# The delta net's inverse: 32-row block products become 128-row products with zeros

## The chip, the cores and the metric

One Trainium2 chip, one of its cores. The metric is the device time of one execution in microseconds (us), as the median of repeated executions. The core has five engines with their own queues: TensorE (PE in the profile, its weight loads PEld), VectorE (DVE), ScalarE (ACT), GpSimd (POOL) and SyncE (SP, which issues most DMAs).

## The reference

The kernel computes a two-layer trunk on a sequence of 1024 positions and width 1024. Layer 0 mixes with a gated delta net, layer 1 with retention; each is followed by a convolutional feed-forward block and layer norms. The change lies in the delta net alone, in its triangular solve:

```python
kk = jnp.where(strict, jnp.einsum('bhncd,bhnmd->bhncm', kb, k) * decay, 0.0)
rhs = jnp.concatenate([v * beta[..., None], kb * jnp.exp(gc)[..., None]], axis=-1)
sol = lax.linalg.triangular_solve(kk + eye, rhs, left_side=True, lower=True, unit_diagonal=True)
...
def step(state, inp):
    v_new = u_n - jnp.einsum('bhck,bhkv->bhcv', w_n, state)
    o = einsum(q_n * exp(g_n), state) + einsum(qk_n, v_new)
    state = state * exp(g_last) + einsum(k_n * exp(g_last - g_n), v_new)
```

There are 8 heads. The reference uses chunks of 64 positions; the kernel uses chunks of 128, so each head has 8 chunks, each with a unit lower triangular matrix of 128x128 to invert. The scan then walks through the chunks of a head one after another.

## The kernel before

All delta net work between the first projections and the output projection (about 60 to 620 us) is written as generators ("streams"): `filler` (projections, each a run of 128x512 products), `t_decay`, `t_path`, `t_chain`, `prep`, `dt_half`, `scan`, `tail`. A small planner, `run` (L727), keeps a clock of its own and picks at each step the stream of highest priority that is due. A stream says after each piece how long it must wait (`yield LAT["t1"]`), which event it needs (`after_ev`), or which buffers (`take`, `give`). Each product adds a cost by the length of its last dimension (`COST = {32: 0.067, 64: 0.119, 128: 0.224, ...}`, in `pm`), and a dependency ties every PE instruction to the one before it (`pq`). So the planner's order is PE's order. The order of the other engines is made by a scheduler from the dependencies.

The inverse of a chunk's matrix is built from its four 32x32 diagonal blocks. `t_path` inverts the diagonal blocks of a quad of four heads on VectorE (lines L894 and L896) and leaves them in two tiles, `RX` and its transposed twin `TX`. `t_chain(p)` (from L915) does the rest for a pair of heads, p = 0 to 3; pairs 0 and 1 run together, pairs 2 and 3 together later. I call these two rounds. `R[h]` holds the inverse in the making, `U[h]` the off-diagonal factors, `T0` the transposed diagonal blocks in columns of 64 per chunk. Its steps:

1. Fill. POOL clears R (L922) and one part of T0 (L937). Blocks of RX go into R's diagonal, blocks of TX into T0. For even p ScalarE copies (L932), for odd p VectorE (L930); two of R's four blocks go by POOL (L952).
2. Step 1 ("T,U 32x32"). For the lower block of each 64-row half, o = 0 and 64: `pa[h3] = U[l3, h3]^T T0[l3]`, one product with 32 rows, 32 columns and 32 columns moved for each head, chunk and half: 32 products in a pair, into one PSUM bank. ScalarE copies the result to `xa` (L967).
3. Step 2 ("R,xa" and "xa,R"). `pb[l3] = xa^T R[h3, h3]` for both halves and `pb[h3] = R[h3, h3]^T xa` for the first: 48 products of 32x32x32 in a pair, all into one bank `pb`. For o = 0 the two kinds alternate; for o = 64 the first kind stands alone. VectorE writes the negated results into T0 (L980, one per head) and R (L984, four per head).
4. Step 3 ("T,U 64x64" and "R,xb 64x64"). The same on 64-row blocks, one bank per head, results by ScalarE to `xb` (L994) and by VectorE into R (L1004).

The banks that steps 1 to 3 use are a pool of two (`mm_tile`, bufs=2). `lane` buffers (four) hold RX, TX, T0 and others; `give("lane", 2)` in t_chain frees RX and TX when both pairs of a quad have passed step 1 of the list above. The event ("T0", p) lets `prep` (transposes of v, shown as "cst,qkv") and `dt_half` ("acc<-qkv 128x128" and "acc<-q,qkv", after a load of DT by SP, which also takes a lane buffer) begin; ("R", p) lets `scan` begin.

Of the kernel before, what the change touches and what calls it, by code (L numbers as in the profile page):

```python
# [12 lines left out]
ALU = mybir.AluOpType  # L13
# [7 lines left out]
NCH = S // P  # L21
# [12 lines left out]
def trunk_kernel(ctx: ExitStack, tc, A):  # L34
    nc = tc.nc
    pe, act, dve, pool, sp = nc.tensor, nc.scalar, nc.vector, nc.gpsimd, nc.sync
# [24 lines left out]
    def mm_tile():  # L61
        return ps.tile([P, HALF], F32, tag="mm", name="mm", bufs=2)
# [13 lines left out]
    def v4(ap):  # L76
        return ap.rearrange("p (c f) -> p c f", f=P)
# [7 lines left out]
    xs = [dr.tile([S, D], F32, tag=f"xs{i}", name=f"xs{i}") for i in range(3)]  # L85
# [612 lines left out]
    U, DT, R, St = {}, {}, {}, {}  # L698
# [4 lines left out]
    events = {}  # L703

    def pq(inst, cost):
        if pin[0] is not None:
            tc.add_manual_dep(inst.ins, pin[0].name,
                              mybir.DependencyInfo(mybir.DependencyClass.NoSync, mybir.DependencyReason.DATA),
                              reason="issue order")
        pin[0] = inst.ins  # L710
        clk[0] += cost
# [3 lines left out]
    def pm(out, lhsT, rhs, start=True, stop=True, cost=None):  # L715
        pq(pe.matmul(out, lhsT, rhs, start=start, stop=stop), cost or COST[out.shape[-1]])  # L716
# [4 lines left out]
    def after_ev(*names):  # L721
        return ("ev", names)

    def emit(name, lat=0.0):
        events[name] = clk[0] + lat
# [40 lines left out]
    def q4s(q4):  # L766
        return slice(q4 * 4, (q4 + 1) * 4)
# [3 lines left out]
    def take(tag, n):  # L771
        while free[tag] < n:
            yield lambda: free[tag] >= n
        free[tag] -= n

    def give(tag, n):
        free[tag] += n
# [131 lines left out]
    def rx(h, n):  # L909
        return R[h][n // 4][:, n % 4 * P:n % 4 * P + P]  # L910
# [4 lines left out]
    def t_chain(p):  # L915
        heads = pairs[p]
        yield after_ev(("X", p // 2))
        yield from take("auh", 4)
        for h in heads:
            R[h] = two("auh", F32, "R")  # L920
            for q4 in range(2):
                pool.memset(R[h][q4], 0.0)  # L922
        yield after_ev(("T", p // 2))
        RX, TX = RTX[p // 2]
        cx = p % 2 * 16
        yield from take("lane", 1)

        def block(out, src):
            if p % 2:
                dve.tensor_copy(out, src)  # L930
            else:
                act.activation(out, src, AF.Copy)  # L932
        T0 = tl("lane", [P, 2, NCH, 64], name="T0")
        lo, hi = slice(0, 64), slice(64, 128)
        for hh, h in enumerate(heads):
            ch = slice(cx + hh * 8, cx + hh * 8 + 8)
            pool.memset(T0[0:32, hh, :, 32:64], 0.0)  # L937
            for b in range(3):
                bs = slice(32 * b, 32 * b + 32)
                cs = slice(32, 64) if b == 1 else slice(0, 32)  # L940
                block(T0[bs, hh, :, cs], TX[bs, :, ch].rearrange("p i c -> p c i"))
        for hh, h in enumerate(heads):
            for q4 in range(2):
                Rv = v4(R[h][q4])
                ch = slice(cx + hh * 8 + q4 * 4, cx + hh * 8 + q4 * 4 + 4)
                for b in range(4):
                    bs = slice(32 * b, 32 * b + 32)
                    src = RX[bs, :, ch].rearrange("p i c -> p c i")
                    if b < 2:
                        block(Rv[bs, :, bs], src)  # L950
                    else:
                        pool.tensor_copy(Rv[bs, :, bs], src)  # L952
        if ("T0", p ^ 1) in events:
            give("lane", 2)
        emit(("T0", p))
        yield LAT["T0"]
        yield from take("t2", 1)
        pa = mm_tile()
        xa = tl("t2", [P, HALF], name="xa")
        for o in (0, 64):  # L960
            l3, h3 = slice(o, o + 32), slice(o + 32, o + 64)
            for hh, h in enumerate(heads):
                for n in range(NCH):
                    c0 = hh * 256 + 32 * n
                    pm(pa[h3, c0:c0 + 32], U[h][l3, n, h3], T0[l3, hh, n, 0:32])
        for o in (0, 64):
            act.activation(xa[o + 32:o + 64], pa[o + 32:o + 64], AF.Copy)  # L967
        yield LAT["t1"]
        pb = mm_tile()
        for o in (0, 64):  # L970
            l3, h3 = slice(o, o + 32), slice(o + 32, o + 64)
            for hh, h in enumerate(heads):
                for n in range(NCH):
                    c0 = hh * 256 + 32 * n
                    pm(pb[l3, c0:c0 + 32], xa[h3, c0:c0 + 32], rx(h, n)[h3, h3])
                    if o == 0:
                        pm(pb[h3, c0:c0 + 32], rx(h, n)[h3, h3], xa[h3, c0:c0 + 32])
        for hh, h in enumerate(heads):
            pv = pb[:, hh * 256:hh * 256 + 256].rearrange("p (c f) -> p c f", f=32)
            dve.tensor_scalar(T0[32:64, hh, :, 0:32], pv[32:64], -1.0, None, ALU.mult)  # L980
            for o in (64, 0):
                l3, h3 = slice(o, o + 32), slice(o + 32, o + 64)
                for q4 in range(2):
                    dve.tensor_scalar(v4(R[h][q4])[l3, :, h3], pv[l3, q4s(q4)], -1.0, None, ALU.mult)  # L984
        give("t2", 1)
        yield LAT["t2"]
        yield from take("t2", 2)
        xb = {}
        for hh, h in enumerate(heads):
            pa = mm_tile()  # L990
            xb[h] = tl("t2", [P, HALF], name="xb")
            for n in range(NCH):
                pm(pa[hi, 64 * n:64 * n + 64], U[h][lo, n, hi], T0[lo, hh, n])
            act.activation(xb[h][hi], pa[hi], AF.Copy)  # L994
        emit(("Ufree", p))
        give("lane", 1)
        yield LAT["t3"]
        for h in heads:
            pb = mm_tile()
            for n in range(NCH):  # L1000
                pm(pb[lo, 64 * n:64 * n + 64], xb[h][hi, 64 * n:64 * n + 64], rx(h, n)[hi, hi])
            pv = pb.rearrange("p (c f) -> p c f", f=64)
            for q4 in range(2):
                dve.tensor_scalar(v4(R[h][q4])[lo, :, hi], pv[lo, q4s(q4)], -1.0, None, ALU.mult)  # L1004
        give("t2", 2)
        emit(("R", p), LAT["mm"])
# [222 lines left out]
    c, z = "c", "z"  # L1229
# [586 lines left out]
    cs = {}  # L1816
# [358 lines left out]
```

## Time and profile before

| what | us |
|---|---|
| median of 3 runs | 2892.94 (2889.35 to 2898.21) |
| the profiled execution, its own time | 2895.01 |
| its span, first to last instruction | 2893.2 |
| PE busy | 2796.5 |
| DVE busy | 2181.8 |
| round 1 of the inverse (pairs 0, 1), steps 1 to 3 | about 261 to 293 |
| round 2 (pairs 2, 3), steps 1 to 3 | about 507 to 541 |
| scan of heads 0 to 3, of heads 4 to 7 | about 304 to 356, 549 to 613 |

In the answers of the trace, a row gives a start and a duration or a busy time; "[x <-y]" is idle time of the engine before the row and what ended it. PEclk is the TensorE clock that was granted, as a share of full speed; a product of fp32 numbers shows as two records on PE, each with a weight load on PEld. A PE record lasts from its start to the modelled end of its results, so records overlap, and the distance between starts tells the rate.

### The profile page before, as it was taken

Reading aid. Unit: us, or ns where it says so; the run is one execution under the profiler, and the core shown is the slowest. Engines: PE = TensorE matmul, PEld = TensorE weight load, DVE = VectorE, ACT = ScalarE, POOL = GpSimd, SP = SyncE. Lnnn points to the kernel's source line nnn. Section 1 sums busy time; section 2 is a strip of 40 time slices with the busy share of each in tenths; the row PEclk is TensorE's granted clock in tenths of the full one; section 3 lists DMA queues with packets and bytes.
Section 4 is the critical chain, followed back from the end, with each engine's and each line's share of the span. In section 5 each row is a group of like instructions: output and inputs, shape, how many; then the busy total and the mean of one; then the engine's idle time right before and its main releaser. Section 6 shows DMA issues by size and latency. Waiting matters only on the chain.

```text
span 2893.2 us, 38921 instructions
## 1 busy us (share of the span) xinstructions
PE 2796.5 (97%) x13594; PEld 2289.9 (79%) x13594; DVE 2181.8 (75%) x3874; ACT 1296.7 (45%) x2387; POOL 484.6 (17%) x509
## 2 busy tenths in 40 slices
PE   7999999999999999999999999999999999999997
PEld 6788887887787777887788887777777788888886
DVE  5787688576788888858687666666789887777779
ACT  4664375344544444545443333222344644444543
POOL 0311231010022333000000001333301023332001
PEclk9998999899999999999999999999999999999999
DMA  7233233174254655845443354665764253434853
GB/s 277 84 99 117 89 129 112 44 241 153 83 179 169 204 181 176 294 150 175 150 142 113 131 197 143 203 188 177 233 221 150 73 197 138 142 132 161 289 182 116
DMA packets 252884, 465.30 MB, mean 161 GB/s; under 512 B 24144, under 2 KB 77776, under 8 KB 252688
## 3 DMA queue, kind: packets, MB, share of 16 engines
q1 hardware_dynamic: 218560, 408.02, 42.8%
q10 hardware_dynamic: 31488, 46.15, 4.3%
q0 software_dynamic: 2640, 8.65, 0.8%
q8 instruction: 107, 1.75, 0.2%
q14 instruction: 89, 0.73, 0.1%
HBM read 346.86 MB, written 115.87 MB: 160 GB/s over the span
## 4 chain that ended last, share of the span: by engine, by line
PE 60%; DVE 21%; DMA 8%; issue 5%; ACT 4%; POOL 1%; SPq 0%; ACTq 0%; DVEq 0%; POOLq 0%
PE acc L716 11%; PE acc L1292 5%; PE acc L1592 4%; PE sc L716 4%; PE acc L110 4%; PE acc L111 4%; PE acc L112 4%; PE mm L716 3%; PE sc L1292 3%; DVE o L1738 2%; DVE wb L90 2%; DMA wr<-in_ffn_up 2%; DMA mvw<-in_ada_w 2%; DVE mm L1346 2%; DVE ada L239 1%
## 5 line engine op out<-in xcount | busy, mean ns | idle before, releaser
L716 PE MATMUL acc<-hT,wh 128*128 128x512 f32 x960 | 301.1, 395 | 0.0
L1592 PE MATMUL acc<-bb,ab 128*128 128x512 f32 x984 | 231.0, 394 | 8.2 <-DVE ab L90 4.4
L89 ACT ACTIVATE ab<-ar 128x512 fp32r<-128x512 f32 x210 | 131.4, 630 | 222.9 <-PE mm L303 49.8
L1592 PEld LDWEIGHTS acc<-bb,ab 128*128 128x128 f32 x984 | 184.2, 189 | 50.0 <-DVE bb L90 4.7
L716 PEld LDWEIGHTS acc<-hT,wh 128*128 128x128 f32 x960 | 183.2, 191 | 36.1
L90 DVE TENSOR_TENSOR ab<-ar,ab 128x512 fp32r<-128x512 f32 x210 | 146.1, 701 | 80.3 <-ACT ab L89 80.1
L1292 PE MATMUL acc<-T,wb 128*128 128x512 f32 x840 | 202.0, 389 | 0.4 <-DVE wb L90 0.4
L716 PE MATMUL acc<-hT,wl 128*128 128x512 f32 x480 | 197.4, 411 | 3.3 <-ACT sq L509 2.1
L89 ACT ACTIVATE wb<-mm 128x512 fp32r<-128x512 f32 x216 | 124.3, 597 | 167.8 <-DVE mm L1346 154.1
L1292 PEld LDWEIGHTS acc<-T,wb 128*128 128x128 f32 x840 | 157.5, 188 | 33.8 <-ACT o L1739 1.2
L90 DVE TENSOR_TENSOR wl<-wr,wh 128x1024 fp32r<-128x1024 f32 x98 | 122.8, 1253 | 76.3 <-ACT wh L89 76.0
L90 DVE TENSOR_TENSOR wb<-wr,wb 128x512 fp32r<-128x512 f32 x162 | 116.3, 719 | 66.1 <-ACT wb L89 66.1
L89 ACT ACTIVATE wh<-wr 128x1024 fp32r<-128x1024 f32 x98 | 103.8, 1060 | 137.4 <-PE acc L716 54.1
L1769 POOL TENSOR_TENSOR o<-o 128x512 f32<-128x512 f32 x80 | 113.0, 1422 | 265.2 <-ACT pc L1362 173.1
L1738 DVE SCALAR_TENSOR_TENSOR o<-g,vc,o 128x512 f32<-128x512 f32 (+2 forms) x176 | 148.3, 852 | 8.2 <-ACT o L1733 7.0
L90 DVE TENSOR_TENSOR wb<-mm,wb 128x512 fp32r<-128x512 f32 x216 | 144.4, 681 | 7.6 <-ACT wb L89 7.6
L89 ACT ACTIVATE wb<-wr 128x512 fp32r<-128x512 f32 x162 | 101.2, 626 | 94.8 <-PE acc L1292 28.5
L1346 DVE TENSOR_TENSOR mm<-wr 128x512 f32<-128x512 f32 x108 | 85.9, 796 | 75.5 <-DMA wr<-in_ffn_up 60.9
L716 PE MATMUL acc<-wh,hT 128*128 128x512 f32 x384 | 134.3, 412 | 1.8 <-DVE vv L90 1.8
L1362 ACT ACTIVATE pc<-acc 128x512 f32<-128x512 f32 x143 | 84.3, 590 | 109.9 <-PE acc L1292 63.4
L239 DVE SCALAR_TENSOR_TENSOR ada<-mvw,e,ada 128x512 f32<-128x512 f32 x140 | 105.3, 752 | 23.4 <-DMA mvw<-in_ada_w 23.0
L110 PE MATMUL acc<-T,wb 128*128 128x512 f32 x292 | 114.4, 392 | 6.1 <-DVE wb L90 6.1
(674 smaller groups left out, 7371.9 us busy)
## 6 DMA issues: line engine op xcount, KB each, us to landing
wr<-in_ffn_up SPq DMA_DIRECT2D x92, 512.0 KB, 3.9
mvw<-in_ada_w SPq DMA_DIRECT2D x80, 512.0 KB, 4.3
ad<-o SPq DMA_DIRECT2D x154, 256.0 KB, 2.3
ar<-ad SPq DMA_DIRECT2D x154, 256.0 KB, 3.9
Br<-in_ffn_down SPq DMA_DIRECT2D x88, 256.0 KB, 3.6
wr<-in_ret_wv SPq DMA_DIRECT2D x32, 512.0 KB, 3.7
ar<-od SPq DMA_DIRECT2D x56, 256.0 KB, 5.2
wr<-in_gdn_wqkv SPq DMA_DIRECT2D x24, 512.0 KB, 3.6
```

The lines of the kernel that those rows point to most:

```text
L89: anchor["sp"] = act.activation(dst_h, src, AF.Copy)
L90: eng.tensor_tensor(dst_l, src, dst_h, ALU.subtract)
L110: mm(acc, wl[:, k], hl[0], start=first, stop=False)
L111: mm(acc, wh[:, k], hl[1], start=False, stop=False)
L112: mm(acc, wh[:, k], hl[0], start=False, stop=last)
L239: dve.scalar_tensor_tensor(a, wr[:, kk], e[:, k:k + 1], a, ALU.mult, ALU.add)
L716: pq(pe.matmul(out, lhsT, rhs, start=start, stop=stop), cost or COST[out.shape[-1]])
L1292: return pe.matmul(*a, skip_group_check=True, **kw)
L1346: dve.tensor_tensor(t, x, y, op)
L1592: return pe.matmul(*args, skip_group_check=True, **kw)
L1738: dve.scalar_tensor_tensor(tv, gv[:, c0 - j:c1 - j], w[:, 2 - j:3 - j], tv, ALU.mult, ALU.add)
L1769: (dve if fp == 0 else pool).tensor_tensor(o[d], o[x], o[y], op)
```

## The change

Only `t_chain` changes.

- T0 is cleared over all 128 rows (POOL, 128x512 per head instead of 32x256), and at first only the blocks of rows 0 to 31 and 64 to 95 are copied in, the second into columns 32 to 63. The remaining block, rows 32 to 63, follows behind step 1.
- Step 1 uses all 128 rows of U and T0: 32 products per pair as before, each with 128 rows, 32 columns of weights and 32 columns moved. What other rows hold meets zeros in T0.
- xa is cleared on POOL first (128x512), so its rows outside the two blocks are zero.
- Step 2 uses all 128 rows, too. One product of xa with two of R's column blocks (64 columns moved) replaces the two products of the halves; the other kind stays. So 16 products in a head, 32 in a pair instead of 48, and they alternate throughout.
- The results of step 2 go into one bank per head instead of one per pair.
- RX and TX are given back behind step 1 and the late block copies, by a new event ("T1", p).

```diff
-            pool.memset(T0[0:32, hh, :, 32:64], 0.0)
-            for b in range(3):
+            pool.memset(T0[:, hh], 0.0)
+            for b in (0, 2):
                 bs = slice(32 * b, 32 * b + 32)
-                cs = slice(32, 64) if b == 1 else slice(0, 32)
-                block(T0[bs, hh, :, cs], TX[bs, :, ch].rearrange("p i c -> p c i"))
+                block(T0[bs, hh, :, 16 * b:16 * b + 32], TX[bs, :, ch].rearrange("p i c -> p c i"))
...
-        if ("T0", p ^ 1) in events:
-            give("lane", 2)
         emit(("T0", p))
...
+        pool.memset(xa, 0.0)
         for o in (0, 64):
-            l3, h3 = slice(o, o + 32), slice(o + 32, o + 64)
+            h3 = slice(o + 32, o + 64)
             for hh, h in enumerate(heads):
                 for n in range(NCH):
                     c0 = hh * 256 + 32 * n
-                    pm(pa[h3, c0:c0 + 32], U[h][l3, n, h3], T0[l3, hh, n, 0:32])
+                    pm(pa[h3, c0:c0 + 32], U[h][:, n, h3], T0[:, hh, n, o // 2:o // 2 + 32])
...
+        for hh in range(2):
+            ch = slice(cx + hh * 8, cx + hh * 8 + 8)
+            block(T0[32:64, hh, :, 32:64], TX[32:64, :, ch].rearrange("p i c -> p c i"))
+        if ("T1", p ^ 1) in events:
+            give("lane", 2)
+        emit(("T1", p))
         yield LAT["t1"]
-        pb = mm_tile()
-        for o in (0, 64):
-            l3, h3 = slice(o, o + 32), slice(o + 32, o + 64)
-            for hh, h in enumerate(heads):
-                for n in range(NCH):
-                    c0 = hh * 256 + 32 * n
-                    pm(pb[l3, c0:c0 + 32], xa[h3, c0:c0 + 32], rx(h, n)[h3, h3])
-                    if o == 0:
-                        pm(pb[h3, c0:c0 + 32], rx(h, n)[h3, h3], xa[h3, c0:c0 + 32])
         for hh, h in enumerate(heads):
-            pv = pb[:, hh * 256:hh * 256 + 256].rearrange("p (c f) -> p c f", f=32)
+            pb = mm_tile()
+            pv = pb.rearrange("p (c f) -> p c f", f=64)
+            for n in range(NCH):
+                xs = xa[:, hh * 256 + 32 * n:hh * 256 + 32 * n + 32]
+                pm(pv[0:32, n], xs, rx(h, n).rearrange("p (b j) -> p b j", j=32)[:, 1::2])
+                pm(pv[32:64, n, 0:32], rx(h, n)[:, 32:64], xs)
...
```

The other rows of the diff are the VectorE writes behind step 2, as many as before and of the same sizes.

What this does to the order on PE at the first round's step 1 stands in the next two fences (T with a number is T0 of a pair, "hT" rows are projections, "cst,qkv" transposes of `prep`, "acc<-qkv" products of `dt_half`). Before:

```order
L716 MATMUL acc<-qkv 128x128 x4
L719 MATMUL acc<-cst,qkv 128x128 x8
L716 MATMUL acc<-hT,wl 128x512
L716 MATMUL acc<-hT,wh 128x512 x2
L716 MATMUL acc<-hT,wl 128x512
L716 MATMUL acc<-hT,wh 128x512 x2
L716 MATMUL acc<-qkv 128x128 x4
L716 MATMUL mm<-T_2178,U 32x32 x32
L716 MATMUL mm<-T_2203,U 32x32 x32
L719 MATMUL acc<-cst,qkv 128x128 x8
L716 MATMUL acc<-hT,wl 128x512
L716 MATMUL acc<-hT,wh 128x512 x2
```

With the change:

```order
L719 MATMUL acc<-cst,qkv 128x128 x8
L716 MATMUL acc<-hT,wl 128x512
L716 MATMUL acc<-hT,wh 128x512 x2
L716 MATMUL acc<-hT,wl 128x512
L716 MATMUL acc<-hT,wh 128x512 x2
L716 MATMUL acc<-hT,wl 128x512
L716 MATMUL acc<-hT,wh 128x512 x2
L719 MATMUL acc<-cst,qkv 128x128 x8
L716 MATMUL acc<-hT,wl 128x512
L716 MATMUL acc<-hT,wh 128x512 x2
L716 MATMUL mm<-T_2178,U 32x32 x32
L716 MATMUL mm<-T_2201,U 32x32 x32
```

The 64 products of step 1 keep their number (the shape shown is that of the result); `dt_half`'s products have moved behind step 2, and transposes and projections ahead of step 1.

ScalarE in the same round, behind its copies into R (L491, L485 and L488 belong to a projection's convolution; "acc" is what a projection left in PSUM). Before:

```order
L485 ACTIVATE raw<-acc 128x512
L488 ACTIVATE oq<-acc,vc 128x512
L932 ACTIVATE T_2178<-TX 32x8x32 x6
L491 ACTIVATE oq<-oq 128x512
L1212 DMA qd<-oq 128x512
L485 ACTIVATE raw<-acc 128x512
L488 ACTIVATE oq<-acc,vc 128x512
L89 ACTIVATE wh<-wr 128x1024
```

With the change:

```order
L485 ACTIVATE raw<-acc 128x512
L488 ACTIVATE oq<-acc,vc 128x512
L491 ACTIVATE oq<-oq 128x512
L932 ACTIVATE T_2178<-TX 32x8x32 x2
L1212 DMA qd<-oq 128x512
L932 ACTIVATE T_2178<-TX 32x8x32 x2
L491 ACTIVATE oq<-oq 128x512
L485 ACTIVATE raw<-acc 128x512
L488 ACTIVATE oq<-acc,vc 128x512
L89 ACTIVATE wh<-wr 128x1024
L1212 DMA qd<-oq 128x512
L932 ACTIVATE T_2178<-TX 32x8x32
```

Two of the six copies into T0 have moved behind step 1, one ahead of each pair's copies to xa, and one L491 has moved ahead of the L485 and L488 that free the next "acc".

PE in the second scan (sc: heads 4 and 5, mm: heads 6 and 7; "qkv,R", "w,DT", "w,U" and "Sn,..." are a chunk's products in turn). Before:

```order
L716 MATMUL sc<-qkv,R 128x128
L716 MATMUL sc<-Sn,qkv 128x128 x2
L716 MATMUL mm<-Sn,qkv 128x128
L716 MATMUL mm<-Sn,q 128x128
L716 MATMUL mm<-Sn,qkv 128x128
L716 MATMUL mm<-Sn,q 128x128
L716 MATMUL sc<-w,DT 128x128
L716 MATMUL sc<-w,U 128x128
L716 MATMUL acc<-hT,wl 128x512
L716 MATMUL acc<-hT,wh 128x512 x2
```

With the change:

```order
L716 MATMUL sc<-Sn,qkv 128x128 x4
L716 MATMUL mm<-Sn,qkv 128x128
L716 MATMUL mm<-Sn,q 128x128
L716 MATMUL mm<-Sn,qkv 128x128
L716 MATMUL mm<-Sn,q 128x128
L716 MATMUL acc<-hT,wl 128x512
L716 MATMUL acc<-hT,wh 128x512 x2
L716 MATMUL sc<-qkv,R 128x128 x2
L716 MATMUL mm<-qkv,R 128x128
```

Before, heads 4 and 5 ran half a chunk apart; with the change they run side by side, as heads 0 to 3 do in the first scan in both kernels, and more of the projections is left for behind the scan. Behind the first products of the output projection PE's order is the same.

More of the change, by code (lines that the diff above doesn't have):

```diff
@@ L964, in t_chain @@
                     c0 = hh * 256 + 32 * n
-                    pm(pa[h3, c0:c0 + 32], U[h][l3, n, h3], T0[l3, hh, n, 0:32])
+                    pm(pa[h3, c0:c0 + 32], U[h][:, n, h3], T0[:, hh, n, o // 2:o // 2 + 32])
         for o in (0, 64):
             act.activation(xa[o + 32:o + 64], pa[o + 32:o + 64], AF.Copy)
-        yield LAT["t1"]
-        pb = mm_tile()
-        for o in (0, 64):
-            l3, h3 = slice(o, o + 32), slice(o + 32, o + 64)
-            for hh, h in enumerate(heads):
-                for n in range(NCH):
-                    c0 = hh * 256 + 32 * n
-                    pm(pb[l3, c0:c0 + 32], xa[h3, c0:c0 + 32], rx(h, n)[h3, h3])
-                    if o == 0:
-                        pm(pb[h3, c0:c0 + 32], rx(h, n)[h3, h3], xa[h3, c0:c0 + 32])
-        for hh, h in enumerate(heads):
-            pv = pb[:, hh * 256:hh * 256 + 256].rearrange("p (c f) -> p c f", f=32)
-            dve.tensor_scalar(T0[32:64, hh, :, 0:32], pv[32:64], -1.0, None, ALU.mult)
-            for o in (64, 0):
-                l3, h3 = slice(o, o + 32), slice(o + 32, o + 64)
+        for hh in range(2):
[4 more added lines that the diff above has]
+        emit(("T1", p))
+        yield LAT["t1"]
+        for hh, h in enumerate(heads):
+            pb = mm_tile()
[4 more added lines that the diff above has]
+                pm(pv[32:64, n, 0:32], rx(h, n)[:, 32:64], xs)
+            dve.tensor_scalar(T0[32:64, hh, :, 0:32], pv[32:64, :, 0:32], -1.0, None, ALU.mult)
+            for o in (32, 0):
                 for q4 in range(2):
-                    dve.tensor_scalar(v4(R[h][q4])[l3, :, h3], pv[l3, q4s(q4)], -1.0, None, ALU.mult)
+                    dve.tensor_scalar(v4(R[h][q4])[2 * o:2 * o + 32, :, 2 * o + 32:2 * o + 64],
+                                      pv[0:32, q4s(q4), o:o + 32], -1.0, None, ALU.mult)
         give("t2", 1)
```

## The prediction

> **What bounds the kernel now.** First the page: the busy times, and the chain that ended last.
>
> ```profile
> PE 2796.5 (97%) x13594; PEld 2289.9 (79%) x13594; DVE 2181.8 (75%) x3874; ACT 1296.7 (45%) x2387; POOL 484.6 (17%) x509
> ...
> PE 60%; DVE 21%; DMA 8%; issue 5%; ACT 4%; POOL 1%; SPq 0%; ACTq 0%; DVEq 0%; POOLq 0%
> ```
>
> PE is busy for 97% of the span and carries most of the chain, so time is gained where PE does the same work faster, and lost where it waits. Next the stretches with their granted clock (columns: stretch and length, busy time and instructions of PE, PEld, DVE, ACT, POOL, then PEclk, DMA share, GB/s).
>
> ```profile
> 240.00:320.00 80.00, 73.47 (x769) 65.37 (x769) 52.68 (x112) 27.82 (x60) 10.13 (x21) 0.89 0.31 102
> 320.00:480.00 160.00, 157.05 (x854) 134.35 (x854) 129.76 (x350) 94.10 (x203) 42.62 (x55) 1.00 0.35 116
> 480.00:620.00 140.00, 132.51 (x1144) 117.60 (x1143) 90.28 (x223) 60.29 (x162) 18.04 (x30) 0.93 0.31 104
> 620.00:2893.00 2273.00, 2213.76 (x9821) 1791.51 (x9819) 1732.64 (x2795) 980.50 (x1701) 375.30 (x339) 1.00 0.51 171
> ```
>
> The clock is full almost everywhere, but not in the two stretches that hold the two rounds of the inverse. Cut at the moments at which it changes, the same view says why:
>
> ```profile
> 134.77:138.18 3.41, 1.35 (x10) 1.31 (x11) 3.19 (x13) 1.18 (x2) 0.00 (x0) 1.00 0.58 230
> 254.25:257.66 3.41, 1.01 (x7) 0.93 (x8) 2.26 (x4) 2.87 (x5) 0.00 (x0) 0.99 0.73 208
> 257.66:261.07 3.41, 3.41 (x13) 2.83 (x11) 3.20 (x5) 0.40 (x1) 0.00 (x0) 0.50 0.70 258
> 261.07:264.48 3.41, 3.41 (x116) 3.38 (x116) 1.74 (x3) 1.20 (x3) 0.00 (x0) 1.00 0.60 192
> 264.48:267.88 3.40, 3.40 (x28) 3.18 (x26) 1.27 (x2) 1.79 (x3) 0.00 (x0) 0.50 0.52 198
> 267.88:271.29 3.41, 3.41 (x172) 3.07 (x171) 1.02 (x4) 0.00 (x0) 0.00 (x0) 1.00 0.43 145
> 271.29:281.53 10.24, 9.56 (x76) 8.57 (x74) 6.62 (x21) 1.18 (x2) 0.00 (x0) 0.50 0.17 57
> 285.02:288.43 3.41, 3.41 (x48) 3.24 (x46) 0.96 (x3) 1.18 (x2) 0.00 (x0) 1.00 0.05 17
> 503.42:506.83 3.41, 1.88 (x16) 1.40 (x15) 2.81 (x5) 1.93 (x10) 0.18 (x1) 1.00 0.31 127
> 506.83:510.24 3.41, 3.41 (x112) 3.24 (x110) 1.05 (x3) 2.65 (x11) 0.00 (x0) 1.00 0.02 5
> 510.24:530.66 20.42, 19.74 (x280) 18.07 (x278) 8.91 (x25) 2.54 (x5) 0.00 (x0) 0.50 0.09 28
> ```
>
> The clock changes on a grid of 3.41 us. Behind 134.77 and 254.25 it fell to half because PE had been busy for 1.35 and 1.01 us of a window; with 1.88 us, from 503.42, it stayed. But it also fell at 264.48, 271.29 and 510.24, behind windows in which PE was busy throughout. What ran there:
>
> ```profile
> 261.10 4.26 PE L716 MATMUL mm<-T,U 32*32 32x32 f32 x128
> 268.22 0.21 PE L716 MATMUL mm<-R,xa 32*32 32x32 f32 x1
> 269.25 1.01 PE L716 MATMUL mm<-R,xa 32*32 32x32 f32 x27
> 271.09 1.60 PE L716 MATMUL mm<-R,xa 32*32 32x32 f32 x29
> 283.30 2.08 PE L716 MATMUL mm<-R,xb 64*64 64x64 f32 x32
> 285.38 2.05 PE L716 MATMUL mm<-T,U 64*64 64x64 f32 x32
> 288.35 1.04 PE L719 MATMUL acc<-cst,qkv 128*128 128x128 f32 x8
> 295.01 1.05 PE L716 MATMUL acc<-qkv 128*128 128x128 f32 x8
> 507.09 4.41 PE L716 MATMUL mm<-T,U 32*32 32x32 f32 x128
> ```
>
> The three windows are filled by 32x32x32 products. Something that sets the clock counts a small product as little work. Two mixed windows of 64x64 products, one of them from 285.02 with 2.3 of 3.41 us of them, kept the clock.
>
> The Trainium skill, page "TensorE: Matmul & The Clock Gate", section "HAM oscillation — how this bites in real kernels", lets the clock fall when PE idles for over about 3.4 us. The windows at 261.07 and 506.83 agree on the length and not on the cause, since PE never idled in them.
>
> **Part 1: the clock.** The change leaves 32 columns of weights but uses 128 rows instead of 32, in steps 1 and 2. What would be counted, the trace doesn't say: if rows in use, a product of the change counts as full (1.0 instead of 0.25); if cells in use, 0.25 instead of 0.06. By the rows above a window of full-size work keeps the clock from a share between 0.40 (1.35 of 3.41) and 0.55 (1.88 of 3.41). So rows would keep it, and cells would not. I take rows: from 267.88 two 32-column blocks ran side by side for a part of the window (64 records from 268.22 to 269.25, 16 ns each, against some 31 ns in the row from 269.25), so more columns were in use, and it fell all the same. That is a leaning, no proof.
>
> What a kept clock is worth: PE's busy time at half clock becomes half. 3.40 + 9.56 + 19.74 = 32.70 us; half is 16.35. The half-clock window from 257.66 follows idle time and stays. Bounds: 0 and 16.4; I take 16.4, and the waits below off it.
>
> **Part 2: the products.** Step 1 keeps 64 products a round (128 records, 33 ns each). Step 2 has 64 products instead of 96. In a head, 8 products move 64 columns; the 32 records from 283.30 with 64 columns take (2.08 − 0.22) / 31 = 0.060 each, so 16 x 0.060 = 0.96 us if the other kind runs beside them, as today, and 1.47 if each waits for the other (16 x 0.032 more). Today a pair takes 64 x 16 + 32 x 31 ns = 2.0 us, 1.0 a head. So 0 at the low end, 0.5 x 8 = 4 at the high end; I take 0, as the two kinds still use different columns.
>
> **Part 3: one bank per head.** Two banks serve, so the third head's step 2 must wait until VectorE has emptied the first's. VectorE and the copies:
>
> ```profile
> 270.37 0.42 DVE L980 TENSOR_SCALAR T<-mm 32x256 f32<-32x256 f32 x1 [2.38 <-PE mm L716]
> 270.80 0.98 DVE L984 TENSOR_SCALAR R<-mm 32x128 f32<-32x128 f32 x4
> 271.80 0.42 DVE L980 TENSOR_SCALAR T<-mm 32x256 f32<-32x256 f32 x1
> 276.31 1.97 PE L716 MATMUL mm<-T,U 64*64 64x64 f32 x16 [0.68 <-ACT xb L994]
> L967 ACT ACTIVATE xa<-mm x8: 587/588/591, 263.2 to 512.1; 32x512 f32<-32x512 f32 x8
> 256.65 0.66 PE L719 MATMUL acc<-cst,qkv 128*128 128x128 f32 x4 [4.24 <-ACT oq L488]
> L932 ACT ACTIVATE T<-TX x12: 629/674/690, 249.3 to 494.9; 32x256 f32<-32x256 f32 x12
> L937 POOL MEMSET T<- x8: 301/302/455, 248.8 to 494.3; 32x256 f32 x8
> L922 POOL MEMSET R<- x16: 522/526/546, 59.1 to 393.6; 128x512 f32 x16
> ```
>
> A head costs VectorE 271.80 − 270.37 = 1.43 us. Counted from the start of step 2: PE does heads one and two until 1.92, VectorE the first until 2.49; PE idles 0.58, does the third until 3.46; VectorE ends the second at 3.92, PE idles 0.49, does the fourth until 4.9. Four `dt_half` products (8 records, 0.9 by the row from 295.01) fill until 5.8; the third bank is free at 5.35, the fourth at 6.78; step 3's first 8 products (half of 2.05) end at 6.8, so both banks come in time. Sum 1.1 us against the 0.68 in the row from 276.31, so 0.4 more in a round, 0.8 in both. Bounds 0 (at half clock PE is behind VectorE) and 3, if VectorE has other work in between.
>
> **Part 4: POOL and ScalarE.** T0's clearing grows from 0.30 to 0.53 us (a clearing of R has the same size), four clearings of xa come in at 0.53 each; POOL is busy for 17% of the span, and ScalarE now turns to L491 first, which covers it. ScalarE's two late copies put 0.67 ahead of each pair's xa: the first pair's is ready 0.67 + 2 x 0.59 = 1.9 us behind its step 1, while PE has 2.1 us of the other pair's step 1 and then 8 transposes and 3 projections (1.04 + 0.7) to do. The second pair's has the same 1.7 and step 2 of the first pair. Nothing, then; without that cover each would cost up to 1.3. The 4.24 us in which PE idles ahead of 256.65 for an L488 on ScalarE stay: four copies and two L491 stand before it in place of six and one. The later give of RX and TX holds back `dt_half`'s loads of DT, whose products stand behind step 2 now and long before the scan; 0, at most 1.
>
> **Part 5: the second scan.** It takes on the pattern that the first has.
>
> ```profile
> 300.00:356.00 56.00, 53.10 (x397) 48.94 (x395) 36.42 (x108) 25.96 (x84) 10.02 (x11) 1.00 0.33 109
> 548.00:600.00 52.00, 50.92 (x381) 47.39 (x381) 31.79 (x94) 24.13 (x81) 4.79 (x4) 1.00 0.25 81
> 600.00:612.00 12.00, 8.95 (x53) 7.26 (x53) 7.15 (x20) 4.12 (x11) 1.01 (x1) 1.00 0.79 256
> ```
>
> PE idles 2.9 us in the first scan and 1.1 in the second: +1.8. The close of the second idles 3.05; more projections are left for behind it, so it may gain or lose 2. I take +1.8, ends −1 and +4.
>
> **Sum.** −16.4 + 0 + 0.8 + 0 + 1.8 = −13.8 us. The profiled execution took 2895.01 and would take 2881.2; the median stands 2.07 lower, so 2879.1.
>
> **Rivals.**
> - *The clock falls all the same*, because cells or columns count: the change doesn't bring what part 1 hopes for. The window from 285.02 speaks neither for nor against it: by cells its 64x64 products count 0.25, and 2.3 of 3.41 us of that with 1.1 of full size make 0.49, which lies above 0.40 too. Then 0.8 + 1.8 remain: 2895.5; with products one after the other and a worse scan close up to 2901.
> - *The clock holds in one round only*, as the grid of 3.41 us falls otherwise over the mix of products and waits: about half of 16.4, so 2892.9 − 8.2 + 2.6 = 2887.3.
> - *Slower: weight loads come into the open.* Each record has its own load. Today's 32x32 loads last 114 ns and hide behind products 33 ns apart:
>
> ```profile
> L716 PEld LDWEIGHTS mm<-T,U 32*32 32x32 f32 x256 | 8.4, 114 | 0.4 <-issue 0.4
> L614 PEld LDWEIGHTS sc<-hT,wab 128*32 128x32 f32 x8 | 0.9, 108 | 1.7 <-DVE hT L90 1.4
> ```
>
>   If a load over all 128 rows can't run beside a product over all rows, each of the 512 records in steps 1 and 2 takes 108 ns; today these steps take 4.3 + 4.5 us in round 1 (from 261.10, and from 268.22 to 272.69) and at most 4.4 + 9 in round 2, with step 2 at half clock. 512 x 0.108 = 55 against 22: +33, about 2926. It decides from 12 ns a record (6.1 us, with the 2.6 above 8.7). Against it: transposes with 128x128 weights come at 1.04 / 8 = 0.13 us each, with 128 columns moved, though their loads also fill all rows.
>
> The Trainium skill, the same page, section "Part 3: Packing small matmuls — row/col tiling", says that a weight load overlaps running products only if its row group differs; by that rule the time would be the 2926. Step 1 contradicts it: all its products of one half sit in the same 32 rows, 33 ns apart.
>
> **How the numbers follow.** The clock holds: 0.50, own range 2875 to 2885 (2892.9 − 16.4 − 1.5, and with 6 us more of waits). It falls: 0.34. One round: 0.07. Weight loads: 0.09. A measurement of this kernel can tell about 0.3%, 8.7 us, from no change. Faster by more: 0.45 of the first case; within: the rest of it, 0.05, with 0.07 and most of the second, 0.31; slower: 0.09 and 0.03 of the second. The range from 2874 to 2900 holds the first three cases but for their ends.
>
> **What would show it.** Right: PEclk 1.0 in the windows of steps 1 to 3; transposes behind step 2 at 1.04 for eight, as from 288.35; short PE waits for VectorE in step 2; a second scan with some 3 us idle. Wrong: PEclk 0.50 behind the "T,U 32x32" rows again; records of steps 1 and 2 over 60 ns apart; a PE wait for xa or for POOL.

## The result and the profile after

The changed kernel takes 2878.12 us (median of 6 runs, 2873.07 to 2881.79) beside 2895.57 for the kernel before (6 runs, 2889.35 to 2899.15): a ratio of 0.9941 with a 95% interval from 0.9924 to 0.9958, or 17.4 us. Measured twice more, each time beside the kernel before on one chip, the ratio was 0.9946 (0.993 to 0.9963) and 0.9945 (0.9931 to 0.9958), about 16 us (15.3 and 14.4 between the medians). The profiled execution took 2881.79 us, with a span of 2880.0 instead of 2893.2.

First the page of the changed kernel, then the answer by stretches with the same columns as in the prediction.

```profile
PE 2784.3 (97%) x13466; PEld 2275.5 (79%) x13466; DVE 2178.8 (76%) x3874; ACT 1297.3 (45%) x2387; POOL 499.3 (17%) x513
```

```profile
240.00:320.00 80.00, 75.00 (x770) 66.73 (x769) 54.53 (x125) 30.94 (x77) 14.69 (x25) 0.98 0.35 114
...
480.00:620.00 140.00, 130.49 (x1122) 115.23 (x1121) 93.73 (x223) 65.56 (x172) 16.92 (x26) 1.00 0.37 130
620.00:2880.00 2260.00, 2202.15 (x9739) 1780.32 (x9737) 1718.42 (x2775) 968.97 (x1682) 385.09 (x338) 0.99 0.51 170
```

PE loses 12.2 us of busy time, and the granted clock of the two stretches with the inverse goes from 0.89 to 0.98 and from 0.93 to 1.00. Cut on the grid of the clock, with one row ahead of step 1 of round 1, three that hold steps 1 and 2 of it, and two of round 2:

```profile
253.70:257.10 3.40, 3.40 (x26) 2.65 (x25) 3.31 (x7) 0.62 (x1) 0.00 (x0) 0.51 0.78 272
257.10:260.50 3.40, 3.40 (x118) 3.38 (x115) 3.33 (x6) 2.15 (x4) 0.00 (x0) 0.99 0.58 162
260.50:263.90 3.40, 3.40 (x75) 2.96 (x73) 2.16 (x6) 2.14 (x4) 0.00 (x0) 1.00 0.35 114
263.90:267.30 3.40, 2.29 (x75) 2.02 (x70) 3.25 (x13) 0.00 (x0) 0.00 (x0) 1.00 0.64 198
497.80:501.20 3.40, 3.40 (x117) 3.40 (x117) 0.62 (x2) 3.15 (x12) 0.00 (x0) 1.00 0.02 7
504.60:508.00 3.40, 2.29 (x78) 2.03 (x74) 3.25 (x12) 0.00 (x0) 0.00 (x0) 1.00 0.18 58
```

Windows full of step 1 (118 and 117 records) no longer bring the clock down, and neither do the windows of step 2, in which PE is busy for only 2.29 of 3.40 us. The half-clock window ahead of step 1, behind an idle PE, is still there. The rows of PE's timeline in step 1 and behind it, and the two waits inside step 2 of round 1:

```profile
256.32 4.28 PE L716 MATMUL mm<-T,U 128*32 128x32 f32 x128
...
264.95 0.22 PE L716 MATMUL mm<-R,xa 128*32 128x64 f32 x1 [0.71 <-DVE R L983]
266.40 0.22 PE L716 MATMUL mm<-R,xa 128*32 128x64 f32 x1 [0.40 <-DVE R L983]
...
268.47 2.07 PE L716 MATMUL mm<-T,U 64*64 64x64 f32 x32
...
497.81 3.94 PE L716 MATMUL mm<-T,U 128*32 128x32 f32 x128
```

The 128-row products come at 3.94 / 128 = 31 ns a record. The rows of step 1 before, 4.26 and 4.41 us, were a little longer because each ends in a half-clock window (from 264.45 and from 510.21). Step 3 (the 64x64 row) no longer waits for xb.

Where the time went is read from one stretch with the same ends in both kernels: from the first record of step 1 in round 1 to the first record of the output projection (L326). Of the kernel before, by the two rounds and the second scan, and as a whole:

```profile
261.10:304.24 43.14, 42.46 (x589) 38.68 (x589) 22.19 (x50) 7.79 (x15) 0.00 (x0) 0.84 0.22 78
304.24:507.09 202.85, 195.63 (x1076) 166.73 (x1075) 163.02 (x422) 117.90 (x267) 52.41 (x78) 1.00 0.35 115
507.09:548.76 41.67, 40.96 (x556) 37.15 (x555) 21.89 (x50) 9.13 (x21) 0.00 (x0) 0.75 0.12 40
548.76:627.90 79.14, 75.02 (x517) 67.66 (x516) 53.53 (x144) 39.68 (x111) 9.59 (x8) 1.00 0.47 160
261.10:627.90 366.80, 354.07 (x2732) 310.21 (x2732) 260.63 (x663) 174.50 (x413) 62.00 (x86) 0.95 0.33 112
```

And of the changed kernel:

```profile
256.32:294.18 37.86, 36.76 (x526) 33.46 (x526) 25.42 (x57) 9.08 (x17) 0.00 (x0) 0.99 0.29 94
294.18:497.81 203.63, 196.08 (x1076) 166.62 (x1074) 163.21 (x419) 117.11 (x265) 53.00 (x80) 1.00 0.34 112
497.81:533.18 35.37, 34.01 (x502) 30.56 (x502) 22.39 (x52) 10.83 (x24) 0.00 (x0) 1.00 0.18 62
533.18:611.60 78.42, 72.49 (x505) 65.42 (x503) 52.52 (x143) 39.40 (x111) 9.15 (x8) 1.00 0.46 162
256.32:611.60 355.28, 339.33 (x2604) 296.06 (x2603) 263.55 (x668) 176.42 (x415) 62.15 (x88) 1.00 0.34 116
```

The stretch is 11.5 us shorter: PE's busy time falls by 14.7, and its idle time (length less busy time) rises from 12.7 to 15.9. In two further profiles of the changed kernel the stretch lasted 354.3 and 353.7 us, so 12.5 and 13.1 less than before; of the kernel before there is one profile. Outside of it the two profiles differ by −4.8 us ahead (256.32 against 261.10) and by +3.1 behind (2268.4 against 2265.3). About 1.5 of the 4.8 belongs to the change (the wait for L488, under POOL and ScalarE below). The rest, and what lies behind, moves between profiles of one and the same kernel too: step 1 began at 256.3, 260.0 and 257.1 us in the three profiles of the changed kernel. Half-clock windows near 45, 58 and 80 us come and go between these three.

### The profile page after: what moved, and what is told of

It is laid out like the page before. It is cut to its first block, busy times and chain, and to the rows that moved or that the text cites. A ratio compares the mean times of both kernels' runs of the same rounds, so it can differ in the third digit from the quotient of the medians.

```text
span 2880.0 us, 38681 instructions
## 1 busy us (share of the span) xinstructions
PE 2784.3 (97%) x13466; PEld 2275.5 (79%) x13466; DVE 2178.8 (76%) x3874; ACT 1297.3 (45%) x2387; POOL 499.3 (17%) x513
## 4 chain that ended last, share of the span: by engine, by line
PE 55%; DVE 21%; DMA 11%; ACT 6%; issue 4%; POOL 1%; SPq 1%; ACTq 0%; DVEq 0%; POOLq 0%
PE acc L716 7%; PE acc L1292 5%; PE acc L1592 4%; PE acc L110 4%; PE acc L111 4%; PE acc L112 4%; PE sc L716 4%; PE sc L1292 3%; DMA mvw<-in_ada_w 3%; PE mm L716 2%; DVE o L1738 2%; DVE qkv L490 2%; DVE wb L90 2%; DVE ada L239 2%; DMA wr<-in_ffn_up 2%
## 5 line engine op out<-in xcount | busy, mean ns | idle before, releaser
L1769 POOL TENSOR_TENSOR o<-o 128x512 f32<-128x512 f32 x80 | 126.3, 1588 | 267.9 <-ACT pc L1362 173.1
```

The source lines that it names most:

```text
L1769: (dve if fp == 0 else pool).tensor_tensor(o[d], o[x], o[y], op)
```

## The experiments

The theory: what holds the clock is the number of rows in use, and the gain is the clock alone. The rivals: cells count; columns count; the new order (one bank per head, late copies, moved products) makes the gain, and the clock follows from it; or the grid fell luckily.

**One shape at a time.** A kernel of its own: thirteen bursts of fp32 products of one shape each, one behind the other, each behind 60 full-size products that bring the clock up. The core of it:

```python
# rows, columns of weights, columns moved, rows of the moving operand that are not zero
BURSTS = [(32,32,32,32), (64,32,32,64), (128,32,32,128), (128,32,32,32), (32,64,32,32), (32,128,32,32),
          (64,64,32,64), (128,64,32,128), (128,128,32,128), (32,32,128,32), (32,128,128,32), (64,64,64,64), (96,32,32,96)]
...
pq(pe.matmul(pt[0:cols, c:c + n], raw[0:rows, k:k + cols], m, start=True, stop=True))
```

> A kernel of its own that computes nothing of the reference: 13 bursts of fp32 products of one shape each (80 to 260 products, planned for some 17 us), each behind 60 full-size products (some 14 us) that bring the clock to 1.0. Shapes as rows x columns of weights, columns moved: 32x32,32; 64x32,32; 128x32,32; 128x32,32 with zeros in 96 of the rows moved; 32x64,32; 32x128,32; 64x64,32; 128x64,32; 128x128,32; 32x32,128; 32x128,128; 64x64,64; 96x32,32. All theories: 32x32 lets the clock fall to 0.50 within two windows of 3.41 us, 128x32 keeps it at 1.0, with or without zeros. If rows in use count: 32x64, 32x128 and the long 32x32 and 32x128 fall too, 128x64 and 128x128 keep it, 64 rows are open. If cells in use count: 32x128 keeps it as 128x32 does (0.25 of the cells each), 64x64 keeps it, 32x64 (0.125) goes as 64x32. Records of one burst come at 30 to 35 ns with 32 columns moved, unless a weight load of 128 rows or 128 columns is slower: then 50 ns or more.

Rows of PE's timeline: start, length, weights as rows*columns, then moving rows x columns; "zm" is the operand that is zero in 96 of 128 rows.

```profile
21.48 24.07 PE L57 MATMUL b<-raw 32*32 32x32 f32 x520
61.92 16.65 PE L57 MATMUL b<-raw 64*32 64x32 f32 x520
92.33 16.65 PE L57 MATMUL b<-raw 128*32 128x32 f32 x520
122.74 16.65 PE L57 MATMUL b<-zm,raw 128*32 128x32 f32 x520
153.14 52.62 PE L57 MATMUL b<-raw 32*64 32x32 f32 x520
222.20 108.50 PE L57 MATMUL b<-raw 32*128 32x32 f32 x520
346.22 51.38 PE L57 MATMUL b<-raw 64*64 64x32 f32 x520
413.72 30.52 PE L57 MATMUL b<-raw 128*64 128x32 f32 x520
457.90 105.35 PE L57 MATMUL b<-raw 128*128 128x32 f32 x520
578.45 29.52 PE L57 MATMUL b<-raw 32*32 32x128 f32 x160
669.52 16.54 PE L57 MATMUL b<-raw 64*64 64x64 f32 x280
```

And the windows of the first burst, before and after the clock fell:

```profile
23.90:27.30 3.40, 3.40 (x112) 3.40 (x109) 0.00 (x0) 0.00 (x0) 0.00 (x0) 0.98 0.02 5
27.30:44.00 16.70, 16.70 (x318) 16.70 (x316) 0.00 (x0) 0.00 (x0) 0.00 (x0) 0.50 0.01 2
```

The clock fell 2.9 to 6.2 us into every burst that has 32 rows (five shapes, with 32, 64 or 128 columns of weights and 32 or 128 moved), and also with 64x64 and 128x128 weights when only 32 columns are moved. It held with 64, 96 and 128 rows of 32 columns, with zeros in three quarters of the rows, with 128x64 weights, and with 64x64 weights when 64 columns are moved. So it isn't columns (32x128 fell), nor cells: 64x32 (an eighth of the array) held and 128x128 (all of it) fell. Nor is it rows alone: by rows, 128x128 was expected to hold. What sets that burst apart is that its products come further apart. From start to start, before the fall, its records stood 112 ns apart, those of 64x64 58, those of 128x64 58, those of 64x32 32. (The counts in the rows of windows include records that began earlier, so length over count comes out a little short.) Records that move 128 columns through 32x32 weights stood 109 ns apart, 0.85 ns for each column. With that, a shape's share is rows/128 times columns moved times 0.85 over the distance. What fell has 0.25 or less (128x128: 0.24; 64x64 with 32 moved: 0.23; the 32-row shapes 0.06 to 0.25). What held has 0.43 or more (64x32: 0.43; 64x64 with 64 moved: 0.47; 128x64: 0.47). That is a rule made after the bursts to fit all thirteen, not a mechanism that a run has shown.

The Trainium skill, page "TensorE: Matmul & The Clock Gate", section "LDWEIGHTS (loading the stationary operand)", gives a weight load a time in ns of its columns divided by 1.2, whatever its rows. The distances here come within 6 ns of it where 32 columns are moved: 112 ns at 128 columns of weights (107 by the page) with 32 rows as with 128, and 58 at 64 columns (53 by the page) with 64 rows as with 128. At 32 columns the records stood 32 ns apart with 32, 64, 96 and 128 rows.

**The new order with 32 rows.** The changed kernel, with its banks and clearings, but the products of steps 1 and 2 over their own 32 rows, so that step 2 again has 96 products a round. PE's order is otherwise the same up to the output projection. On ScalarE the two late copies stand ahead of step 1 again, since its 32 rows no longer read what they overwrite.

```diff
-                    pm(pa[h3, c0:c0 + 32], U[h][:, n, h3], T0[:, hh, n, o // 2:o // 2 + 32])
+                    pm(pa[h3, c0:c0 + 32], U[h][o:o + 32, n, h3], T0[o:o + 32, hh, n, o // 2:o // 2 + 32])
...
-            for n in range(NCH):
-                xs = xa[:, hh * 256 + 32 * n:hh * 256 + 32 * n + 32]
-                pm(pv[0:32, n], xs, rx(h, n).rearrange("p (b j) -> p b j", j=32)[:, 1::2])
-                pm(pv[32:64, n, 0:32], rx(h, n)[:, 32:64], xs)
+            for o in (0, 64):
+                h3 = slice(o + 32, o + 64)
+                for n in range(NCH):
+                    xs = xa[h3, hh * 256 + 32 * n:hh * 256 + 32 * n + 32]
+                    pm(pv[o:o + 32, n, 0:32], xs, rx(h, n)[h3, h3], cost=0.062)
+                    if o == 0:
+                        pm(pv[32:64, n, 0:32], rx(h, n)[h3, h3], xs, cost=0.062)
```

> The changed kernel with its order on PE, its two banks per pair, its clearings and late copies, but steps 1 and 2 over 32 rows as before (24 products a head in step 2, planned at the same cost). If the rows keep the clock: PEclk falls to 0.50 behind step 1 in both rounds, the time goes back by 11 to 16 us, to 2889 to 2894. If the gain is in the new order, the banks or the moved copies: PEclk may fall or not, the time stays at 2876 to 2882.

2895.44 us beside 2890.37, a ratio of 1.0004 (0.9987 to 1.002); the median is 1.4 us above the range that was expected. The windows of the clock, and the stretch from step 1 to the output projection:

```profile
264.70:268.10 3.40, 3.40 (x25) 2.97 (x22) 1.55 (x3) 1.81 (x3) 0.00 (x0) 0.50 0.28 111
271.50:285.10 13.60, 13.60 (x138) 12.70 (x132) 6.35 (x18) 1.55 (x3) 0.00 (x0) 0.50 0.17 58
513.70:517.10 3.40, 3.40 (x33) 3.24 (x31) 1.11 (x2) 1.30 (x3) 0.00 (x0) 0.52 0.02 5
520.70:534.20 13.50, 13.50 (x139) 12.29 (x132) 5.75 (x17) 1.19 (x2) 0.00 (x0) 0.50 0.13 42
...
261.18:629.87 368.69, 354.07 (x2731) 309.94 (x2731) 263.21 (x664) 174.27 (x413) 62.40 (x88) 0.95 0.32 111
```

The half clock is back in both rounds, and PE's busy time in the stretch is the 354.07 us of the kernel before. The new order alone costs 1.9 us of idle time there (14.6 against 12.7). So the gain comes with the 128-row products. In step 2 these are also fewer, 64 in place of 96 a round; this run undoes both and doesn't separate them.

**One step alone at 32 rows.** The first of the two edits above (step 1), then the second (step 2), each by itself.

> The changed kernel with step 1 alone back at 32 rows. If rows count: the clock falls at the window behind step 1 in both rounds and comes back at the earliest one or two windows later; a loss of 3 to 10 us against the changed kernel, its time at 2880 to 2888. If step 2 alone mattered: no fall.

> The changed kernel with step 2 alone back at 32 rows. Step 2 with its waits for banks fills some 5 us, one or two windows. If rows count: the clock holds through step 1 and falls behind step 2, a loss of 3 to 10 us. If step 1 alone mattered: no fall, 2876 to 2882.

One run each: 2885.84 us with step 1 at 32 rows, 2881.1 with step 2. The clock of step 1's kernel, and its stretch:

```profile
253.80:267.20 13.40, 12.56 (x150) 11.20 (x150) 8.04 (x14) 4.72 (x8) 0.00 (x0) 0.50 0.44 150
506.30:513.20 6.90, 6.90 (x91) 6.09 (x90) 1.38 (x2) 2.11 (x4) 0.00 (x0) 0.51 0.01 2
...
257.82:618.70 360.88, 345.72 (x2604) 302.02 (x2603) 263.02 (x664) 174.53 (x413) 62.67 (x88) 0.98 0.33 114
```

And of step 2's kernel:

```profile
266.90:276.70 9.80, 9.80 (x59) 9.26 (x60) 4.21 (x10) 1.19 (x2) 0.00 (x0) 0.50 0.30 107
512.50:522.60 10.10, 10.10 (x56) 9.08 (x56) 3.46 (x8) 1.19 (x2) 0.00 (x0) 0.50 0.16 54
...
255.57:618.67 363.10, 348.71 (x2732) 304.98 (x2731) 264.10 (x668) 176.09 (x415) 61.62 (x88) 0.97 0.33 114
```

Either step with 32 rows costs the clock by itself, for 7 to 10 us in a round. Step 2 brought it down in both rounds, for 10.2 us each. Step 1 brought it down in round 2, for 6.8 us. In round 1 it didn't fall behind step 1, as had been expected: it was at half already, since PE had waited for ScalarE (busy for 0.15 us of the window from 250.27, and for 2.45 of the next), and two windows with step 1's products kept it there for 6.8 us more of the 13.4 in the first row. Their stretches stand at 6.5 and 8.7 us above the 354.4 that the changed kernel has on the mean of its three profiles: each part of the change is needed, and together the two account for it (15.1 against the 14.3 of both undone, with one profile for each).

**64 rows.** As the kernel with 32 rows, but each product takes its own 32 rows and the 32 beside them, which meet zeros.

```diff
-                    pm(pa[h3, c0:c0 + 32], U[h][o:o + 32, n, h3], T0[o:o + 32, hh, n, o // 2:o // 2 + 32])
+                    pm(pa[h3, c0:c0 + 32], U[h][o:o + 64, n, h3], T0[o:o + 64, hh, n, o // 2:o // 2 + 32])
...
-                    pm(pv[o:o + 32, n, 0:32], xs, rx(h, n)[h3, h3], cost=0.062)
+                    pm(pv[o:o + 32, n, 0:32], xs, rx(h, n)[o:o + 64, h3], cost=0.062)
```

> Steps 1 and 2 over 64 rows in place of 128 (block products that take their own 32 rows and the 32 of zeros beside them; 96 products a round in step 2, as before the change). If the clock counts rows in use and 64 are enough, as the bursts of single shapes say, PEclk stays 1.0 in both rounds and the ratio is that of the changed kernel, 0.994. If in the kernel, with its waits between the products, 64 rows count too little, half clock shows behind the T,U rows in both rounds and the ratio is near 1.000, as with 32 rows.

2887.93 us beside 2891.82, a ratio of 0.9982 (0.997 to 0.9994): neither of the two that were expected, but a third of the gain. The ten runs lie between 2880.95 and 2890.98 us and the profile is of the shortest, so what the clock did in the others isn't shown. The windows of round 1 and one of round 2:

```profile
257.30:260.70 3.40, 3.40 (x120) 3.40 (x121) 3.40 (x5) 1.18 (x2) 0.00 (x0) 1.00 0.63 195
260.70:264.10 3.40, 3.40 (x105) 2.95 (x105) 1.67 (x4) 1.81 (x3) 0.00 (x0) 1.00 0.36 141
264.10:267.50 3.40, 2.26 (x112) 2.10 (x106) 3.25 (x13) 0.00 (x0) 0.00 (x0) 0.98 0.47 169
267.50:277.70 10.20, 10.20 (x82) 9.79 (x78) 4.22 (x13) 1.19 (x2) 0.00 (x0) 0.50 0.19 68
...
509.60:513.00 3.40, 2.62 (x141) 2.54 (x139) 2.43 (x9) 0.00 (x0) 0.00 (x0) 1.00 0.00 0
```

Step 1 at 64 rows kept the clock, as in the burst. Step 2 lost it in round 1, behind a window in which PE waited for banks and was busy for 2.26 us, and kept it in round 2, where such a window had 2.62. With 128 rows the same waits leave 2.29 us busy, and the clock holds. The share that was made for the bursts fits these windows, too. Counted from the starts of the records in them (0.85 ns for each column, 0.42 in the 512-column products), it is 0.39 in the window behind which the clock fell, 0.54 in the one of round 2, and 0.83 and 0.85 in the changed kernel's (from 263.90 and 504.60). So 64 rows stand close to the point where it falls, and a wait of a microsecond can decide.

**The changed kernel again.** Unaltered; a second profile.

> The changed kernel unaltered, for comparison on the same chip as the next three, and as a second profile of it. If the rows in use carry the gain, no window of steps 1 and 2 shows half clock here either, the ratio to the kernel before is 0.994 again (0.992 to 0.996), and the half clock that is left lies behind PE idle times. If the first profile was lucky in how the 3.41 us grid fell, half clock shows in one of the two rounds this time.

2876.5 us, 0.9946 (0.993 to 0.9963). No half clock in steps 1 to 3 but for the idle-caused window that reaches 1.5 us into step 1 of round 1 (258.1 to 261.5). So the full clock there didn't hang on how the grid fell in the first profile.

**Step 1 in another order.** The 128-row products of the two halves, which differ in their columns, are issued in turns.

```diff
-        for o in (0, 64):
-            h3 = slice(o + 32, o + 64)
-            for hh, h in enumerate(heads):
-                for n in range(NCH):
+        for hh, h in enumerate(heads):
+            for n in range(NCH):
+                for o in (0, 64):
+                    h3 = slice(o + 32, o + 64)
```

> Only the order in which step 1 issues its products is changed: for each chunk the product for rows 32 to 63 of the result and then the one for rows 96 to 127, which use different columns, in place of all of the one kind and then all of the other. If products over the same 128 rows run side by side when their columns differ, the 128 records of step 1 take 2.1 us in place of 4.26 in each round; PE has work all the time, so the time falls by some 4 us (2874 beside 2878, ratio to before 0.9925). If products over the same rows can't run side by side at 32 columns moved, or weight loads over 128 rows set the pitch (nothing in step 2 of the changed kernel came below 28 ns a record), they take 3.6 to 4.3 us and the time does not change (0.994).

The row of step 1 in round 2:

```profile
499.72 2.22 PE L716 MATMUL mm<-T,U 128*32 128x32 f32 x128
```

2.22 us instead of 3.94, 17 ns a record (2.94 in round 1, which began at half clock): products over the same 128 rows do run side by side, and weight loads keep up. The stretch is 351.3 us, 3.1 less than the changed kernel's mean. The median, 2875.57 us (0.9943, 0.9925 to 0.9961), can't be told from the changed kernel's 2876.5. In round 2 a new wait for xa (0.8 us) took back part of it.

**Four banks, without and with that order.** The second head of each pair takes its bank for step 2 from the scan's pool of banks.

```diff
-            pb = mm_tile()
+            pb = sc_tile() if hh else mm_tile()
```

> The changed kernel with its own order of step 1, and four banks for step 2's results in place of two. If PE waits for banks in step 2 and nothing else takes the wait's place, the step loses its gaps, as with the new order of step 1, and the stretch from step 1 to the output projection is some 2 to 3 us shorter than in the changed kernel. If the run with both edits owed its 6 us to the order of step 1, or to both only together, the stretch is within 1 us of the changed kernel's. The ratio to the kernel before would be 0.9935 to 0.9945, which alone can't tell the two apart.

> The order of step 1 as in the run before, and the second head of each pair takes its bank for step 2's results from the other group of banks, so that four banks serve and not two. If the banks are what PE waits for in step 2, its four heads follow each other without the two gaps of 0.4 to 0.9 us of the changed kernel, step 2 takes 3.7 to 4.0 us in round 1 in place of 5.1, and the time falls by a further 2 us (ratio to before 0.992). If VectorE's pace is what counts, since step 3 needs all results, the wait turns up ahead of step 3 (T,U 64x64) instead, and nothing is gained (0.9925 to 0.994, as the run before).

> The run with both edits once more, beside the changed kernel on the same chip: if its trace told the truth, the stretch from step 1 to the output projection is 6 us shorter than the changed kernel's, and the ratio to the kernel before 0.992 to 0.9935 where the changed kernel has 0.994 to 0.995. If the first trace of it was lucky in its windows of half clock, the two ratios are the same.

> The changed kernel unaltered, to compare the two others with on the same chip: 0.994 to 0.995 of the kernel before, no half clock in steps 1 to 3 of either round.

The waits of PE between 250 and 640 us in the changed kernel, third profile (what waits, who ends it, sum, times, longest), first three rows:

```profile
PE mm L716 <- ACT qkv L1079: 3.9, 4, 1.6
PE acc L719 <- ACT oq L488: 3.1, 1, 3.1
PE mm L716 <- DVE R L983: 2.2, 4, 0.7
```

And with both edits, second run, first two:

```profile
PE mm L716 <- ACT qkv L1079: 3.9, 4, 1.6
PE acc L719 <- ACT oq L488: 3.3, 1, 3.3
```

The four bank waits are gone and no other took their place. In the third profile of the changed kernel no window of steps 1 to 3 came to half clock but the one behind the idle PE. That one, from 256.4 to 259.8, covers the first 2.8 us of step 1, where no half clock at all had been expected. The stretch lasts 351.5 us with four banks alone, and 347.8 and 346.8 with both edits, against 355.3, 354.3 and 353.7 of the changed kernel: 2.9 us for the banks, 3.1 for the order, 7.1 for both. The times say less: 2874.59 us with the banks (0.9944, 0.9924 to 0.9963), 2874.64 and 2872.57 with both (0.9937, 0.9919 to 0.9956; 0.9942, 0.9926 to 0.9957), beside 2876.5 and 2874.71 for the changed kernel. With both edits the medians lie 2 us lower, but the ratios miss what was expected (0.992, then 0.992 to 0.9935) and the intervals overlap with the changed kernel's. The version with both edits has the shortest stretch, 7 us below the changed kernel's. That its whole runs are the shortest isn't shown: the time at which step 1 begins alone moves by 3.7 us between profiles of one kernel.

## Why the prediction was right, step by step

The forecast was 2879.1 us and the sum −13.8; the median came out at 2878.1, and the profile at −13.2 with −11.5 to −13.1 in the stretch that the terms speak of. That the medians agree to 1 us is in part luck. The forecast started from 2892.94, the median of three runs, where the six runs beside the result have 2895.57; and the medians then differ by 17.4 and not by 13.8. The two errors nearly cancel.

- **Clock, −16.4.** The reading had been called a leaning, and it held: rows count, though not alone, since 128x128 weights fell. Cells and columns are ruled out by the bursts, and the kernel with 32 rows shows that the new order doesn't bring the gain. Of the rivals, the clock that falls all the same didn't come; the one that holds in one round only is what the profile with 64 rows gives. The size was too large. PE's busy time in the stretch fell by 14.7 us (14.2 and 13.9 in the other two profiles), and that includes what step 2 saves with fewer products. The term halved the busy time at half clock, but from start to start a record of 32 columns takes 31.7 ns at full and 53.3 at half clock (first burst), 1.68 times as long; with 128 columns moved it is 109 and 213, 1.95 times. If all of the 32.7 us at half clock were records of 32 columns, they would give back 0.41 of it and not 0.50: 13.3 in place of 16.4.
- **Products, 0.** Step 1's records stand 31 ns apart, step 2 takes some 0.9 us a head (8 x 2 products, the two kinds side by side). The rival of weight loads in the open is gone: but for the bank waits, no two records of steps 1 and 2 came over 75 ns apart. Step 1 in its other order goes further: products over the same rows come at 17 ns. The rule of the Trainium skill that was weighed there ("TensorE: Matmul & The Clock Gate", section "Part 3: Packing small matmuls — row/col tiling") doesn't hold here.
- **Banks, +0.8.** Two waits in each round, 0.71 and 0.40 us, where 0.58 and 0.49 were worked out; 2.2 us in all. The two waits for xb that they replace summed to 1.4. This term is right to 0.1 us, and the kernels with four banks show that it can be had back.
- **POOL and ScalarE, 0.** No wait for POOL or xa came up. One part was wrong: PE's wait for the L488 on ScalarE was to stay at 4.24 us. In the three profiles of the changed kernel it is 2.8, 3.2 and 3.1. The two late copies can't run before step 1 has read the zeros that they replace, so they no longer stand ahead of L488 on ScalarE. Where step 1 reads 32 or 64 rows, all six copies stand there again and the wait is 3.9 to 4.2 (the kernels with 32 rows, with 64 rows, and with step 1 alone at 32). That is 1.1 to 1.5 us of gain that the sum lacked, though its own price of 0.67 for a copy would have given 1.3 for the two.
- **Second scan, +1.8.** PE's idle time from its start to the output projection rose from 4.1 to 5.9 us in the first profile and to 4.8 in the second (77.53 us long, 72.71 busy), and in the third it was 3.9 (76.56 long, 72.67 busy). The stretch itself did not grow, since 2.5 us of PE's work had been moved ahead of it. So the term came out between −0.2 and +1.8; that the first profile gives the forecast value is luck.

The errors have both signs: the clock term about 2 us too large, the L488 wait missed by 1.1 to 1.5 us, the second scan up to 2 us too dear. The stretch and the L488 wait make 13 to 14.2 us in the three profiles; what is left of the 14 to 17 us between the medians no run here assigns.

## What to carry to other kernels

Small products can bring TensorE's clock down while it is busy all the time: look for PEclk 0.50 behind windows with full PE, and ask how many rows the products there use, and for what share of the time they move columns. Widening a product over zeros to all rows cost PE nothing here, as the columns stayed the same, and kept the clock in both rounds; 64 rows were too close to the edge to survive a wait. Once that is done, issue products in turns that use different columns, and give them banks enough; but read such a gain in a stretch with fixed ends, since the time of a whole run moves by more.

## What the runs showed that was not expected

- A full-size array isn't enough: 128x128 weights with 32 columns moved fell to half clock, where its records stand 112 ns apart.
- At half clock a record of 32 columns takes 1.68 times as long (31.7 and 53.3 ns), not twice.
- 64 rows of 32 columns held the clock in a burst of their own and in step 1, and lost it in step 2 behind a window with 1.1 us of waits.
- Two products over the same 128 rows, in different columns, run side by side at 17 ns a record.
